# A fixed set of seven-product row pairs for every MLP product, with a new order of the weight blocks and three-part additions to x

## The chip, the cores and the metric

The kernel runs on one core of a Trainium2 chip. The metric is the device time of one execution in microseconds (us); where several runs are given, the median counts. Engines: PE is TensorE (matmuls), DVE is VectorE, ACT is ScalarE, POOL is GpSimd, SP issues the DMAs of the weights.

## The reference

A decoder trunk of two layers over 256 rows of 2048 float32 values: a retention layer and a latent-attention layer, each followed by an MLP. The MLPs are what the change is about:

```
def rms_norm(x, gain):
    return x * rsqrt(mean(x * x) + 1e-6) * gain

def sq_relu_mlp(h, w1, w2):            # w1: 2048 x 8192, w2: 8192 x 2048
    return square(relu(h @ w1)) @ w2

for layer in range(2):
    x = x + (retention(h) if layer == 0 else mla_attention(h))   # h = rms_norm(x, ...)
    x = x + sq_relu_mlp(rms_norm(x, norm_mlp[layer]), mlp_w1[layer], mlp_w2[layer])
```

## The kernel before, in words

**Splitting.** Every float32 operand is split into a high part (rounded to fp32r) and a low part, the rest. `split` (L182) does it: ScalarE casts (L185), VectorE subtracts (L186). A product of two operands is three matmuls: high by high, high by low, low by high (L354 to L356).

**Pair products.** `gemm_pair` (L331) multiplies the 256 rows of activations by one *column pair* of a weight: 1024 columns. The inner dimension is taken in *row pairs* of 256 weight rows. `quad` (L282) handles one row pair: it loads one 1 MB chunk (128 partitions x 2048 values, four blocks of 512 columns b11, b22, b12, b21, L285) and multiplies the 2 x 2 blocks of the activations by the 2 x 2 blocks of the weight. An *eight* does it in eight products of 128 x 128 by 128 x 512 and splits the chunk in two halves of 1024. A *seven* does it in seven products, in Strassen's manner (Winograd's form): it splits b11 with b22, then b21 alone, then adds blocks in place on VectorE (L319, L322, L323) and splits the four results u1 to u4 in two halves. It also needs sums of the activation's blocks, made beforehand by `with_sums` (L390): three subtractions or additions, and a split.

Split weights lie in rings of five buffers each, "wh" and "wl", of 128 x 1024; raw chunks lie in a ring of four. The accumulators c11, c12, c21, c22 take the four banks "acc" of PSUM, p1 and p5 the two banks "tp" that the transposes use too, p6 and p7 the two banks "at". When a pair product ends, `pair_out` (L366) copies six of them out on ScalarE (L371) and combines p1, p5, p6, p7 on VectorE: L373, L374, and one tick later L377, L378.

**The MLP.** `mlp` (L782) works in four groups of 2048 hidden columns. A group has two pair products of w1, called U1 and U2 here (p even and p odd; tiles named u_), of 8 row pairs each, and then two of w2, D1 and D2 (tiles named d_), of 8 row pairs each, over the group's eight hidden tiles. When a U ends, `up` adds the two parts of each block (`summed`, L387), scales and clips (L795), transposes on TensorE (L205), squares (L804), splits, and makes four hidden tiles; those that meet a seven get their sums at once (L807). So U1's hidden tiles are made during U2, and U2's during D1. In the first three groups the results of D1 and D2 go to x in DRAM by accumulating DMAs on POOL's queue, two parts for each of four blocks of each row half (`to_home`, L145). In the last group they are added on VectorE to x in SBUF (`into_x`, L152; L461), and, in layer 0, squared, transposed and split for the next stage while D2 runs. In layer 1 the last D2 is done by plain products with whole hidden tiles (L824).

**Which row pairs are sevens.** THREE is (3, 5, 7), FOUR is (1, 3, 5, 7), HEAD is (2, 4, 6, 7), counted from 0. U1 has FOUR (layer 0's first U1 the last two of THREE, layer 1's first U1 all of THREE); U2 has THREE. D1 has THREE; D2 has FOUR in the first three groups and THREE in layer 0's last. So a group has 4 + 3 + 3 + 4. The retention stage's pair products, whose tiles are named rp_, use HEAD already.

**Order.** A list of steps due at a clock that counts row pairs (`later`, `tick`, L99 to L110) sets the order of the program's text; the framework orders the instructions of each engine by it, and waits are by semaphores. In the trace, steps of a pair product's end stand interleaved with the next one's splits.

Of the kernel before, what the change touches and what calls it, by code (L numbers as in the profile page):

```python
# [20 lines left out]
P = 128  # L21
# [47 lines left out]
def yoco(ctx: ExitStack, tc: tile.TileContext, a):  # L69
# [212 lines left out]
    def quad(w, chunk, x, mm, name):  # L282
# [11 lines left out]
        def parts(src, n, part):  # L294
# [3 lines left out]
            return [[i[:, j * 512 : (j + 1) * 512] for i in (wh, wl)] for j in range(n)]  # L298

        if more is None:  # L300
            b11, b22 = parts(raw[:, 0:1024], 2, 0)
# [4 lines left out]
            b12, b21 = parts(raw[:, 1024:], 2, 1)  # L306
# [5 lines left out]
        b11, b22 = parts(raw[:, 0:1024], 2, 0)  # L312
# [5 lines left out]
        b = raw.rearrange("p (i n) -> p i n", i=4)  # L318
        nc.vector.tensor_tensor(  # L319
            b[:, 0:3:2], b[:, 0:2], b[:, 2].unsqueeze(1).to_broadcast([P, 2, 512]), op=ALU.add  # L320
        )
        nc.vector.tensor_tensor(b[:, 1], b[:, 0], b[:, 1], op=ALU.add)  # L322
        nc.vector.tensor_tensor(b[:, 3], b[:, 1], b[:, 3], op=ALU.add)  # L323
# [7 lines left out]
    def gemm_pair(w, chunk0, act, kinds, name, done):  # L331
# [26 lines left out]
        for i in range(len(kinds)):  # L358
# [3 lines left out]
            if i == len(kinds) - 1:  # L362
                queue.append((clock[0] + 1, -1, lambda: pair_out(made, name, done)))
            tick()

    def pair_out(c, name, done):  # L366
# [9 lines left out]
        def rest():  # L376
            nc.vector.tensor_tensor(v, o["p5"], v, op=ALU.subtract)  # L377
            nc.vector.tensor_tensor(o["p5"], o["p5"], u, op=ALU.subtract)  # L378
            done([[(o["c11"], o["p1"]), (o["c12"], v)], [(o["c21"], u), (o["c22"], o["p5"])]])
# [48 lines left out]
    def x_block_t(blocks, b, g0s, outs, name, sums):  # L428

        for k2 in range(2):  # L430
# [3 lines left out]
            for g0, out in zip(g0s, outs):  # L434
# [5 lines left out]
                elif 2 * b + k2 in FOUR:  # L440
# [341 lines left out]
    def mlp(layer, act, r, done):  # L782
        w1, w2 = a[f"mlp_w1_{layer}"], a[f"mlp_w2_{layer}"]
        f0 = 0
        for gi, nf in enumerate(GROUPS):
            hid, blocks = [], []
            last = gi == len(GROUPS) - 1

            def up(c, p, hid=hid, blocks=blocks, last=last):
# [7 lines left out]
                def turn(i):  # L797
                    for q in (2 * i, 2 * i + 1):
# [8 lines left out]
                        blocks.append((v, with_sums(u, name) if len(blocks) in (THREE if last else FOUR) else None))  # L807
# [376 lines left out]
```

## Time and profile before

| what | value |
|---|---|
| median of 3 runs | 2479.52 us (2478.8 to 2480.16) |
| the profiled execution's own time | 2477.67 us |
| its span, first to last instruction | 2475.9 us |
| granted TensorE clock | 1.00 |
| layer 0's MLP in the trace | about 729 to 1409 us |
| layer 1's MLP in the trace | about 1792 to 2471 us |

The views used below: the page (busy time of the engines, 40 slices, the chain of work that ended last); windows (busy time of each engine in a stretch, with the number of instructions in brackets); groups of instructions (line, engine, operation, out<-in, shapes, count, busy time in us, mean duration of one in ns, idle time before them and what ended it); the timeline (start, duration, instruction; equal neighbours are merged, with a count; in square brackets the engine's idle time before it and what ended that); and waits. Instructions of one engine overlap a little, so a group's busy time is below count times mean.

### The profile page before, as it was taken

To read this page: it belongs to the slowest core of one execution; us is meant where nothing else is said; L and a number is where in the kernel's file an instruction comes from. 1 tells how busy PE (TensorE), PEld (TensorE's weight loads), DVE (VectorE), ACT (ScalarE), POOL (GpSimd) and SP (SyncE) were. 2 spreads that over 40 slices of the span, in tenths; PEclk is the share of its full clock that TensorE was granted. 3 is DMA by queue.
4 is the path that set the end of the run, shared out by engine and by line. 5 is a ranking of instruction groups with operands and counts; after the bars stand their busy time and mean duration, and the time that the engine had idled before them with its cause. 6 is when DMAs were issued, how large, how long until landed. Compare 5 with 4: busy or idle time off the path is not lost.

```text
span 2475.9 us, 31725 instructions
## 1 busy us (share of the span) xinstructions
PE 2457.9 (99%) x11638; PEld 2061.5 (83%) x11638; DVE 2158.9 (87%) x2800; ACT 1592.6 (64%) x2251; POOL 249.6 (10%) x310
## 2 busy tenths in 40 slices
PE   9999999999999999999999999999999999999999
PEld 7888888888888888888888888998888888888887
DVE  7799989889899999999999967776689999999996
ACT  6566655555676667667666766576566666676663
POOL 7400011000000010110110001110000201101100
PEclk9999999999999999999999999999999999999999
DMA  9645468556564685674785564445645956857854
GB/s 324 214 173 206 172 207 253 189 184 220 195 226 182 211 265 210 208 259 174 245 266 203 187 231 166 157 154 174 199 173 203 261 214 206 269 201 222 270 192 153
DMA packets 93404, 521.05 MB, mean 210 GB/s; under 512 B 11072, under 2 KB 12224, under 8 KB 40000
## 3 DMA queue, kind: packets, MB, share of 16 engines
q1 hardware_dynamic: 71856, 472.83, 53.0%
q0 software_dynamic: 21248, 46.15, 9.0%
q8 instruction: 91, 1.49, 0.2%
q14 instruction: 65, 0.53, 0.1%
q10 hardware_dynamic: 144, 0.05, 0.0%
HBM read 479.14 MB, written 39.85 MB: 210 GB/s over the span
## 4 chain that ended last, share of the span: by engine, by line
PE 93%; DVE 4%; ACT 2%; issue 1%; POOL 1%; DMA 0%; SPq 0%; ACTq 0%; DVEq 0%; POOLq 0%
PE u_c L354 7%; PE u_c L356 7%; PE u_c L355 7%; PE d_c L356 6%; PE d_c L354 6%; PE d_c L355 6%; PE rp_c L354 3%; PE rp_c L355 3%; PE rp_c L356 2%; PE rk_acc L274 2%; PE rq_acc L274 2%; PE u_p L354 2%; PE u_p L356 2%; PE u_p L355 2%; PE d_p L354 2%; PE d_p L356 2%
## 5 line engine op out<-in xcount | busy, mean ns | idle before, releaser
L185 ACT CAST u_wh<-u_raw 128x1024 fp32r<-128x1024 f32 x362 | 342.2, 990 | 214.1 <-DVE u_raw L322 155.3
L185 ACT CAST d_wh<-d_raw 128x1024 fp32r<-128x1024 f32 x358 | 337.9, 992 | 203.8 <-DVE d_raw L322 164.3
L186 DVE TENSOR_TENSOR u_wl<-u_raw,u_wh 128x1024 fp32r<-128x1024 f32 x362 | 396.8, 1143 | 52.0 <-ACT u_wh L185 50.7
L186 DVE TENSOR_TENSOR d_wl<-d_raw,d_wh 128x1024 fp32r<-128x1024 f32 x358 | 392.4, 1145 | 42.0 <-ACT d_wh L185 41.5
L354 PE MATMUL u_c<-u_wh,n 128*128 128x512 f32 x706 | 276.4, 392 | 0.0
L355 PE MATMUL u_c<-u_wl,n 128*128 128x512 f32 x706 | 275.6, 390 | 0.0
L356 PE MATMUL u_c<-u_wh,n 128*128 128x512 f32 x706 | 274.9, 389 | 0.0
L354 PE MATMUL d_c<-d_wh,hid 128*128 128x512 f32 x654 | 256.0, 391 | 0.0
L355 PE MATMUL d_c<-d_wl,hid 128*128 128x512 f32 x654 | 255.3, 390 | 0.0
L356 PE MATMUL d_c<-d_wh,hid 128*128 128x512 f32 x654 | 254.7, 389 | 0.0
L185 ACT CAST rp_wh<-rp_raw 128x1024 fp32r<-128x1024 f32 (+1 forms) x166 | 158.9, 981 | 147.1 <-DVE rp_raw L322 73.1
L186 DVE TENSOR_TENSOR rp_wl<-rp_raw,rp_wh 128x1024 fp32r<-128x1024 f32 (+1 forms) x166 | 182.5, 1136 | 31.1 <-ACT rp_wh L185 29.5
L356 PEld LDWEIGHTS u_c<-u_wh,n 128*128 128x128 f32 x706 | 132.6, 188 | 27.5
L354 PEld LDWEIGHTS u_c<-u_wh,n 128*128 128x128 f32 x706 | 132.6, 188 | 26.9
L355 PEld LDWEIGHTS u_c<-u_wl,n 128*128 128x128 f32 x706 | 132.6, 188 | 26.6
L356 PEld LDWEIGHTS d_c<-d_wh,hid 128*128 128x128 f32 x654 | 122.8, 188 | 25.4
L354 PEld LDWEIGHTS d_c<-d_wh,hid 128*128 128x128 f32 x654 | 122.8, 188 | 25.0
L355 PEld LDWEIGHTS d_c<-d_wl,hid 128*128 128x128 f32 x654 | 122.9, 188 | 24.8
L150 POOL DMA_DIRECT2D xh<-d_c x48 | 41.6, 867 | 856.1 <-ACT d_c L371 854.2
L185 ACT CAST ro_wh<-ro_raw 128x1024 fp32r<-128x1024 f32 x86 | 83.1, 998 | 59.0 <-DVE ro_raw L322 30.4
L354 PE MATMUL rp_c<-rp_wh,a 128*128 128x512 f32 x286 | 112.0, 392 | 1.1 <-DVE rk_u L624 1.1
L356 PE MATMUL rp_c<-rp_wh,a 128*128 128x512 f32 x286 | 111.4, 390 | 0.0
(465 smaller groups left out, 6070.7 us busy)
## 6 DMA issues: line engine op xcount, KB each, us to landing
u_raw<-in_mlp_w SPq DMA_DIRECT2D x128, 1024.0 KB, 5.7
d_raw<-in_mlp_w SPq DMA_DIRECT2D x120, 1024.0 KB, 5.1
rp_raw<-in_ret_w_gv SPq DMA_DIRECT2D x56, 1024.0 KB, 4.9
ro_raw<-in_ret_w_out SPq DMA_DIRECT2D x32, 1024.0 KB, 4.8
uq_raw<-in_mla_w_uq SPq DMA_DIRECT2D x24, 768.0 KB, 4.1
rq_raw<-in_ret_w_qk SPq DMA_DIRECT2D x16, 1024.0 KB, 5.2
rk_raw<-in_ret_w_qk SPq DMA_DIRECT2D x16, 1024.0 KB, 4.8
wo_raw<-in_mla_w_o SPq DMA_DIRECT2D x16, 1024.0 KB, 4.8
```

Source lines behind the costliest of these rows:

```text
L150: nc.gpsimd.dma_start(x_home[t][2 * p + j], part, accum_op=ALU.add)
L185: nc.scalar.copy(h, src)
L186: nc.vector.tensor_tensor(l, src, h.bitcast(F32), op=ALU.subtract)
L274: nc.tensor.matmul(acc[f], wh[:, cols], a.rearrange("p i s -> p (i s)"), start=k == 0, stop=k == nk - 1)
L354: nc.tensor.matmul(dst, ah, bh, start=n == 0, stop=False)
L355: nc.tensor.matmul(dst, ah, bl, start=False, stop=False)
L356: nc.tensor.matmul(dst, al, bh, start=False, stop=n == total[key] - 1)
```

## The change

Five things, all in the MLPs' pair products or in `quad`, which the retention stage's pair products use too.

1. Every pair product of the MLPs takes HEAD, row pairs 3, 5, 7, 8 counted from 1, as its sevens: 4 + 4 + 4 + 4 in a group. The exceptions are layer 0's first U1 (row pairs 7, 8) and layer 1's first U1 (5, 7, 8), and layer 1's last D2, which is as it was. The sums of x's blocks that U needs are made for HEAD too.
2. The weight's blocks lie as b11, b12, b22, b21. An eight splits blocks 0 and 2, then 1 and 3; a seven splits 0 and 2, then 3.
3. In a seven the first add gives u1 and u3 together, the second u2, the third u4. The splits are u1 with u3, then u2 with u4; the products go p5, p7, p6, c21.
4. In the first three groups, D1's and D2's results leave L377 and L378 out: ScalarE negates u and v, and the blocks of the second column half go to x in three parts.
5. The sums of hidden tiles are separate steps: of tile k, due max(k - 4, 0) ticks after the tile. `blocks` is now a `Pairs` (L25), whose length counts a tile that needs sums when they are there.

```diff
-            wh = pool.tile([P, 1024], F32R, tag="wh", bufs=5, name=f"{name}_wh{part}")
-            wl = pool.tile([P, 1024], F32R, tag="wl", bufs=5, name=f"{name}_wl{part}")
-            split(wh[:, : n * 512], wl[:, : n * 512], src)
+            n = src.free_size() // 512
+            wh, wl = (
+                pool.tile([P, 2, 512], F32R, tag=f"w{i}", bufs=5, name=f"{name}_w{i}{part}")[:, :n] for i in "hl"
+            )
+            split(wh, wl, src)
...
+        b11, b22 = parts(b[:, 0:3:2], 0)
         if more is None:
...
-            b12, b21 = parts(raw[:, 1024:], 2, 1)
+            b12, b21 = parts(b[:, 1:4:2], 1)
...
-        (b21,) = parts(raw[:, 1536:], 1, 1)
+        (b21,) = parts(b[:, 3:4], 1)
         mm("c11", a(0, 1), b21)
         nc.vector.tensor_tensor(
-            b[:, 0:3:2], b[:, 0:2], b[:, 2].unsqueeze(1).to_broadcast([P, 2, 512]), op=ALU.add
+            b[:, 0:2], b[:, 0:3:2], b[:, 1].unsqueeze(1).to_broadcast([P, 2, 512]), op=ALU.add
         )
-        nc.vector.tensor_tensor(b[:, 1], b[:, 0], b[:, 1], op=ALU.add)
-        nc.vector.tensor_tensor(b[:, 3], b[:, 1], b[:, 3], op=ALU.add)
-        u1, u2 = parts(raw[:, 0:1024], 2, 2)
+        nc.vector.tensor_tensor(b[:, 2], b[:, 0], b[:, 2], op=ALU.add)
+        nc.vector.tensor_tensor(b[:, 3], b[:, 2], b[:, 3], op=ALU.add)
+        u1, u3 = parts(b[:, 0:2], 2)
         mm("p5", s(1), u1)
+        mm("p7", s(0), u3)
+        u2, u4 = parts(b[:, 2:4], 3)
         mm("p6", s(2), u2)
-        u3, u4 = parts(raw[:, 1024:], 2, 3)
-        mm("p7", s(0), u3)
         mm("c21", a(1, 1), u4)
...
         def rest():
+            if loose:
+                less = f2k([512], f"{name}_n")
+                nc.scalar.activation(less, u, AF.Copy, scale=-1.0)
+                nc.scalar.activation(v, v, AF.Copy, scale=-1.0)
+                done([[(o["c11"], o["p1"]), (o["c12"], o["p5"], v)], [(o["c21"], u), (o["c22"], o["p5"], less)]])
+                return
             nc.vector.tensor_tensor(v, o["p5"], v, op=ALU.subtract)
             nc.vector.tensor_tensor(o["p5"], o["p5"], u, op=ALU.subtract)
...
-                elif 2 * b + k2 in FOUR:
+                elif 2 * b + k2 in HEAD:
...
-            hid, blocks = [], []
+            hid, sums = [], []
             last = gi == len(GROUPS) - 1
+            kinds = HEAD
+            blocks = Pairs(hid, sums, kinds)
...
-                        blocks.append((v, with_sums(u, name) if len(blocks) in (THREE if last else FOUR) else None))
+                        k = len(hid)
                         hid.append(v)
+                        sums.append(None)
+                        if k in kinds:
+                            def sum_up(k=k, u=u, name=name):
+                                sums[k] = with_sums(u, name)
+                            later(max(k - 4, 0), sum_up)
...
-                kinds = THREE[not (p or layer) :] if p % 2 or not p else FOUR
+                sevens = HEAD if p else HEAD[2 - layer :]
...
-                kinds = [i in (FOUR if p and not last else THREE) for i in range(2 * nf)]
-                gemm_pair(w2, p * 32 + 2 * f0, blocks, kinds, f"d{layer}_{gi}{p}", add)
+                gemm_pair(
+                    w2, p * 32 + 2 * f0, blocks, [i in kinds for i in range(2 * nf)], f"d{layer}_{gi}{p}", add, not last
+                )
...
-    w = np.stack([w[:, :, :, 0, 0], w[:, :, :, 1, 1], w[:, :, :, 0, 1], w[:, :, :, 1, 0]], axis=3)
+    w = np.stack([w[:, :, :, 0, 0], w[:, :, :, 0, 1], w[:, :, :, 1, 1], w[:, :, :, 1, 0]], axis=3)
```

More of the change, by code (lines that the diff above doesn't have):

```diff
@@ L362, in gemm_pair, with pair_out @@
             if i == len(kinds) - 1:
-                queue.append((clock[0] + 1, -1, lambda: pair_out(made, name, done)))
+                queue.append((clock[0] + 1, -1, lambda: pair_out(made, name, done, loose)))
             tick()
-    def pair_out(c, name, done):
+    def pair_out(c, name, done, loose):
         o = {}
@@ L785, in mlp, with up @@
         for gi, nf in enumerate(GROUPS):
-            hid, blocks = [], []
+            hid, sums = [], []
             last = gi == len(GROUPS) - 1
-            def up(c, p, hid=hid, blocks=blocks, last=last):
+            kinds = HEAD
+            blocks = Pairs(hid, sums, kinds)
+            def up(c, p, hid=hid, sums=sums, kinds=kinds):
                 need(r, NT)
@@ L813, in mlp @@
             for p in range(f0 // 2, (f0 + nf) // 2):
-                kinds = THREE[not (p or layer) :] if p % 2 or not p else FOUR
+                sevens = HEAD if p else HEAD[2 - layer :]
                 gemm_pair(
-                    w1, p * 8, act, [i in kinds for i in range(8)], f"u{layer}_{p}", lambda c, p=p, up=up: up(c, p)
+                    w1, p * 8, act, [i in sevens for i in range(8)], f"u{layer}_{p}", lambda c, p=p, up=up: up(c, p)
                 )
```

10 lines of the change are left out of this document (4 added, 6 removed).

## The prediction

> **What bounds the kernel now.** I read the page first: the busy line, the slices, the chain of work that ended last.
>
> ```profile
> span 2475.9 us, 31725 instructions
> PE 2457.9 (99%) x11638; PEld 2061.5 (83%) x11638; DVE 2158.9 (87%) x2800; ACT 1592.6 (64%) x2251; POOL 249.6 (10%) x310
> DVE  7799989889899999999999967776689999999996
> PE 93%; DVE 4%; ACT 2%; issue 1%; POOL 1%; DMA 0%; SPq 0%; ACTq 0%; DVEq 0%; POOLq 0%
> ```
>
> TensorE (PE) holds 93% of the chain. VectorE (DVE) is at 87% on average, but at nine tenths in most slices of the two MLP stretches, so the question is what it has left where the change puts work. An MLP group is four pair products of 8 row pairs each: U1, U2 (w1) and D1, D2 (w2). The timeline of TensorE where a U2 ends and a D1 begins gives the rate of a matmul and the place of the boundary (start, duration):
>
> ```profile
> 985.02 0.39 PE L354 MATMUL u_c<-u_wh,n 128*128 128x512 f32 x1
> 985.25 0.39 PE L355 MATMUL u_c<-u_wl,n 128*128 128x512 f32 x1
> 985.47 0.39 PE L356 MATMUL u_c<-u_wh,n 128*128 128x512 f32 x1
> 985.70 0.39 PE L354 MATMUL d_c<-d_wh,hid 128*128 128x512 f32 x1
> ```
>
> Matmuls start every 0.227 us, 0.68 us for a product's three. Then the windows of one pair product each: of a retention pair, U1, U2, D1, D2 of layer 0's second group, and layer 0's last D2 (length, then PE, PEld, DVE, ACT, POOL busy, clock, DMA share):
>
> ```profile
> 597.80:640.60 42.80, 42.72 (x191) 35.04 (x190) 38.16 (x48) 24.29 (x31) 0.00 (x0) 1.00 0.48 176
> 901.40:942.20 40.80, 40.80 (x182) 33.74 (x181) 37.96 (x41) 25.01 (x31) 4.37 (x5) 1.00 0.83 263
> 942.20:985.70 43.50, 43.50 (x200) 35.86 (x199) 41.17 (x52) 31.12 (x43) 0.00 (x0) 1.00 0.53 190
> 985.70:1029.20 43.50, 43.50 (x200) 35.89 (x199) 41.20 (x52) 31.14 (x43) 2.59 (x3) 1.00 0.53 188
> 1029.20:1070.10 40.90, 40.90 (x182) 33.82 (x181) 38.07 (x41) 25.09 (x31) 6.99 (x8) 1.00 0.87 261
> 1366.60:1409.20 42.60, 42.60 (x193) 35.11 (x192) 41.45 (x53) 28.86 (x45) 2.17 (x4) 1.00 0.54 185
> ```
>
> TensorE is never idle in the MLP windows. VectorE is busy 38 of 41 us in U1 and D2, which have four sevens, and 41.2 of 43.5 in U2 and D1, which have only three: there it also does the combining, the halves' sums and the hidden tiles of the U before. U2 and D1 are the heavy pairs, with 2.3 us of VectorE to spare.
>
> **What the change takes from TensorE.** A seven saves one product. Counted from the code: 26 + 27 sevens in w1 now, 30 + 31 after; 27 + 24 in w2 now, 32 + 28 after. The first add of each seven has its own row, and the counts agree:
>
> ```profile
> L319 DVE TENSOR_TENSOR u_raw<-u_raw 128x1024 f32<-128x1024 f32 x53 | 64.6, 1219 | 0.0
> ...
> L319 DVE TENSOR_TENSOR d_raw<-d_raw 128x1024 f32<-128x1024 f32 x51 | 62.2, 1219 | 0.0
> ```
>
> Seventeen more sevens, 17 x 0.68 = **11.6 us less** of TensorE. Eight are in a U2 and eight in a D1, one each per group; the last is in layer 0's last D2. U1 and other D2s keep their number.
>
> **What it puts on VectorE.** The end of D1 shows what a seven costs (timeline of VectorE):
>
> ```profile
> 1013.86 6.37 DVE L186 TENSOR_TENSOR d_wl<-d_raw,d_wh 128x1024 fp32r<-128x1024 f32 x6 [0.47 <-ACT d_wh L185]
> 1020.15 1.22 DVE L319 TENSOR_TENSOR d_raw<-d_raw 128x1024 f32<-128x1024 f32 x1
> 1021.40 0.69 DVE L322 TENSOR_TENSOR d_raw<-d_raw 128x512 f32<-128x512 f32 x1
> 1022.13 0.69 DVE L323 TENSOR_TENSOR d_raw<-d_raw 128x512 f32<-128x512 f32 x1
> 1023.29 3.71 DVE L186 TENSOR_TENSOR d_wl<-d_raw,d_wh 128x1024 fp32r<-128x1024 f32 x3 [0.47 <-ACT d_wh L185]
> ```
>
> The first row holds five full subtracts and a half one: (6.37 - 0.69) / 5 = 1.14 us each, and the next starts 0.60 after the half one. The adds follow at 1.25 and 0.73 when each waits for the one before, at 1.14 and 0.60 when other work stands between. An eight takes 2 x 1.14; a seven takes 1.14 + 0.60, the adds 1.14 to 1.25, 0.60 to 0.73 and 0.60, and 2 x 1.14. The difference is 4.1 to 4.3; I take **4.2**. The cast of a half block stands in ScalarE's groups:
>
> ```profile
> L185 ACT CAST d_wh<-d_raw 128x1024 fp32r<-128x1024 f32 x307 | 309.2, 1053 | 202.6 <-DVE d_raw L322 164.3 <-PE d_acc L248 16.6 <-PE d_c L356 9.7
> ```
>
> The wait of 0.47 for it goes: u1 and u3 are ready after the first add, so ScalarE casts (1.05 us) while VectorE does the other two (1.33). I count only busy time, so this needs no term: it is time that VectorE gets to use. The layout itself (strided halves of equal length) I take at nothing: this first add has a strided output already, at 1.22. If strides cost or saved 0.05 on each of 5 operations, that is 0.25 per seven, inside the range.
>
> Sums of hidden tiles, by group (means of one):
>
> ```profile
> L186 DVE TENSOR_TENSOR hid_more<-hid_sum,hid_more 128x512 fp32r<-128x512 f32 x30 | 20.6, 686 | 0.0
> ...
> L394 DVE TENSOR_TENSOR hid_sum<-hid_u 128x256 f32<-128x256 f32 x30 | 12.6, 420 | 0.0
> ...
> L378 DVE TENSOR_TENSOR d_p<-d_p,d_u 128x512 f32<-128x512 f32 x15 | 10.3, 687 | 0.0
> ...
> L396 DVE TENSOR_TENSOR hid_sum<-hid_u,hid_sum 128x128 f32<-128x128 f32 x30 | 8.6, 286 | 0.0
> ```
>
> One sum is 0.69 + 0.42 + 2 x 0.29 (L395 has L396's shape), less 0.08 overlap each: 1.34. Now U2 makes two of a group's sums and D1 two (positions 2, 4 and 6, 8). After, positions 3, 5, 7, 8 need them: one in U2, **three in D1**. Deferring the last ones by some row pairs keeps them in D1.
>
> The three-part additions take L377 and L378 (0.60 each by spacing) off VectorE and give ScalarE, busy for 25 of 41 us in such a pair, two negations. But they are of D1's result, done in D2, and of D2's, done in the next U1: the light pairs, where nothing waits for VectorE. So no gain; without them VectorE would need 38.1 of 40.9 there.
>
> **The sum, group by group.** VectorE after: U1 37.96 - 1.2 = 36.8; U2 41.17 + 4.2 - 1.34 = 44.0; D1 41.20 + 4.2 + 1.34 = 46.7; D2 38.07 - 1.2 = 36.9. TensorE: 40.8, 42.8, 42.8, 40.9. Over a group VectorE has 164.4 against 167.3 and would fit, if it could work ahead. How far it can shows before 985.70 and at the end of D1:
>
> ```profile
> 982.27 1.22 DVE L186 TENSOR_TENSOR d_wl<-d_raw,d_wh 128x1024 fp32r<-128x1024 f32 x1 [0.15 <-ACT d_wh L185]
> 984.07 1.23 DVE L186 TENSOR_TENSOR d_wl<-d_raw,d_wh 128x1024 fp32r<-128x1024 f32 x1 [0.57 <-ACT d_wh L185]
> 985.50 2.36 DVE L186 TENSOR_TENSOR d_wl<-d_raw,d_wh 128x1024 fp32r<-128x1024 f32 x2 [0.21 <-ACT d_wh L185]
> ```
>
> ```profile
> 1027.85 0.39 PE L354 MATMUL d_p<-d_wh,hid_more 128*128 128x512 f32 x1
> 1028.07 0.39 PE L355 MATMUL d_p<-d_wl,hid_more 128*128 128x512 f32 x1
> ```
>
> When TensorE starts D1, VectorE has done 1.22 + 1.23 + 0.20 = 2.65 us of D1's splits, with waits for casts between: there are five wh and five wl buffers, the ending seven holds four, and casts wait for the rest. That lead is all a light pair can hand on. At the other end the last split must be done 1.14 us before the pair ends (1028.07 against 1029.21); now it is done at 1023.29 + 1.14 + 1.22 = 1025.65, 2.4 early.
>
> After the change: U2 has 42.8 - 1.14 + 2.65 = 44.3 for 44.0, so it just fits, 0.3 early. VectorE then starts D1 only 1.4 before TensorE and has 43.1 for 46.7: **TensorE waits 3.7 us in each D1** (2.3 if the whole lead survived and a seven costs 4.1; 4.9 if half a us of other waits comes in and U2 stalls too). D2 then gives VectorE 4 us back and the lead returns, capped as before. Eight groups: 8 x 3.7 = 29.6. One new wait lies inside this one. The first seven of a heavy pair comes one row pair (5.4 us) earlier, and its p1 and p5 take the banks that the hidden tiles' transposes use. The last square that reads them in D1, and now's first p1:
>
> ```profile
> 999.87 0.60 ACT L804 ACTIVATE hid_u<-hid_tp 128x512 f32<-128x512 f32 x1
> ...
> 1004.05 0.39 PE L354 MATMUL d_p<-d_wh,hid 128*128 128x512 f32 x1
> ```
>
> p5, three products behind p1, would come at 1004.05 - 5.4 + 2.0 = 1000.6 and the square ends at 1000.47: between nothing and some 1.5 us of wait in TensorE's order, which VectorE uses to catch up. I add nothing. In U1 of each layer's first group, fewer sevens leave more room; the later order of row sums of x I take at nothing there.
>
> Layer 0's last D2 also carries the additions to x and their transposes. Its last split and the matmul that needs it:
>
> ```profile
> 1403.23 2.36 DVE L186 TENSOR_TENSOR d_wl<-d_raw,d_wh 128x1024 fp32r<-128x1024 f32 x2 [0.47 <-ACT d_wh L185]
> ```
>
> ```profile
> 1408.04 0.39 PE L355 MATMUL d_p<-d_wl,hid_more 128*128 128x512 f32 x1
> ```
>
> It is 2.45 early. One more seven (4.2), less two cast waits that vanish (0.9), plus TensorE's 0.68 less, plus the lead lost (2.65 - 1.14), less 2.45: 3.0 us of wait. Sum: 29.6 + 3.0 - 11.6 = **+21.0** on the profiled execution's 2477.67, 2498.7; the median of the runs shown stands 1.85 above it, so **2500.5**. By the bounds, 8 x 2.3 + 1.5 and 8 x 4.9 + 4 for the waits: 2488 to 2511.
>
> [...]
>
> **Rivals.** (a) VectorE keeps up, and the time falls. The engines' orders interleave pieces of several steps, as the rows above do; if U2's combining and sums come to stand so that D1 starts with a larger lead than mine, the wait per group shrinks. It decides at 11.6 / 8 = 1.45 us: D1's VectorE work under 44.5 with the lead as worked out. With no waits at all: 2479.52 - 11.6 = 2467.9. For it: VectorE's total fits over a group, and the retention window above runs four sevens in this very order (two at the end) with TensorE at 42.72 of 42.80. Against it: that window holds only 38.2 us of VectorE. Chance 0.18; another 0.10 that it half works (waits of 1.45 to 2.3, 2475 to 2488).
>
> (b) Transfers. Ten accumulating DMAs in place of eight after each D of the first three groups, three to one place of x, where each waits for the one before. The first half of D2, POOL's waits, and these DMAs' time to landing:
>
> ```profile
> 1029.20:1050.00 20.80, 20.80 (x93) 17.18 (x92) 20.27 (x23) 12.61 (x16) 4.40 (x5) 1.00 0.99 266
> ```
>
> ```profile
> POOL xh L150 <- DMA xh<-d_c: 14.5, 2, 7.3
> ```
>
> ```profile
> DMA to landing us min/median/max: 3.9/8.4/13.9
> ```
>
> The third part starts some 8 us later, so the busy stretch grows longer rather than denser: (0.87 - 0.53) x 40.9 / 8 = 1.7 us a DMA, 3.5 for two, and 0.87 x 40.9 + 3.5 = 39.1 of 40.9. Still under the pair. If weights came late by 2 us in each of the 12 light pairs, beyond the 4 us of VectorE's slack, the time would be 2525. Chance 0.07.
>
> (c) VectorE's operations no longer overlap, each waiting out the one before: U2 53 x 0.085 = 4.5 and D1 61 x 0.085 = 5.2 more. U2 then waits for 44.0 + 4.5 - 44.3 = 4.2 and D1, with no lead but the last 1.14, for 46.7 + 5.2 - 42.8 = 9.1, so 8 x 13.3 + 3.0 - 11.6 = 98 on 2479.5, some 2577. The x6 row nearly excludes it: 0.01. [...] (d) The number of sevens does not grow, 2479.5: 0.02; the lists of kinds say it does.
>
> **How the numbers follow.** Forecast 0.62, rival (a) 0.18 and 0.10, (b) 0.07, (c) 0.01, (d) 0.02. A difference under 0.2% (5 us) is about what a measurement of this kernel can't tell from none. Faster is (a): 0.18. Same (2474.6 to 2484.5) is six of the ten hundredths of the half case, and (d): 0.08. Slower: 0.74. The forecast alone holds 2488 to 2511; down to 2472 it takes in the half case and part of (a), and up to 2512 nothing of (b). About 0.18 stays outside.
>
> **What the profile would show.** Right: the first add counted 61 and 60 times; D1 windows of 45 to 48 us with VectorE over 97% busy and TensorE idle before L355 for the subtract of L186; U2 near 43; U1 and D2 as now with VectorE at nine tenths; no cast waits of 0.47 behind the third add. Wrong: TensorE idle in U1 or D2, or before a weight load for a DMA; D1 under 44.3; a seven's adds or splits off 1.14 and 0.60. What would make it wrong is a lead above 2.65 us at the start of D1, or VectorE work of D1 that I count there and that runs elsewhere.

## The result, and the profile after

| | before | after |
|---|---|---|
| median of the runs shown together | 2479.16 us (2478.31 to 2480.16, 4 runs) | 2545.32 us (2542.22 to 2545.82, 4 runs) |
| ratio, 95% interval | | 1.0267 (1.0255 to 1.0279) |
| the profiled execution's own time | 2477.67 us | 2545.73 us |

The change makes the kernel 66 us slower. The direction was predicted; the size (2500.5, and 2512 as the upper end) was not. The page of the changed kernel: span, busy time, VectorE's slices, the chain of work that ended last.

```profile
span 2543.6 us, 31798 instructions
...
PE 2485.6 (98%) x11587; PEld 2052.6 (81%) x11587; DVE 2228.6 (88%) x2869; ACT 1639.2 (64%) x2311; POOL 270.3 (11%) x334
...
DVE  7799989889989999999999967775699999999995
...
PE 67%; DVE 20%; ACT 7%; issue 4%; DMA 1%; POOL 0%; ACTq 0%; SPq 0%; DVEq 0%; POOLq 0%
```

TensorE held 93% of the chain; now VectorE holds 20% and ScalarE 7%. VectorE's share of the span is only one point higher, 88% for 87%: the average hardly moved, and the chain did. The first add of a seven, by group, of the changed kernel:

```profile
L321 DVE TENSOR_TENSOR u_raw<-u_raw 128x1024 f32<-128x1024 f32 x61 | 74.4, 1220 | 0.0
L321 DVE TENSOR_TENSOR d_raw<-d_raw 128x1024 f32<-128x1024 f32 x60 | 73.3, 1222 | 0.0
```

61 and 60, as counted; TensorE's matmuls fall from 11638 to 11587, by 51, three for each of 17 products. The windows of the changed kernel, one pair each: U1, U2, D1, D2 of layer 0's second group, then D1 and D2 of its last (length, then PE, PEld, DVE, ACT, POOL busy, clock, DMA share, GB/s):

```profile
908.30:949.60 41.30, 41.13 (x181) 33.63 (x180) 37.34 (x39) 26.58 (x33) 6.10 (x7) 1.00 0.84 261
949.60:994.70 45.10, 44.13 (x197) 34.92 (x197) 44.26 (x53) 32.05 (x44) 0.00 (x0) 1.00 0.52 187
994.70:1042.80 48.10, 44.70 (x197) 34.99 (x196) 46.92 (x61) 33.26 (x47) 2.59 (x3) 1.00 0.56 185
1042.80:1083.70 40.90, 40.90 (x182) 33.68 (x180) 37.17 (x39) 26.41 (x32) 8.11 (x10) 1.00 0.87 266
1345.80:1396.30 50.50, 45.48 (x193) 34.89 (x192) 48.47 (x64) 33.96 (x47) 0.00 (x0) 0.98 0.45 165
1396.30:1442.10 45.80, 43.71 (x191) 34.66 (x189) 44.31 (x56) 29.18 (x47) 2.17 (x4) 0.99 0.50 179
```

VectorE's busy times, 37.3, 44.3, 46.9 and 37.2, are those of the prediction (36.8, 44.0, 46.7, 36.9) within 0.6 us. But U2 lasts 45.1 against 42.8 of TensorE's own, D1 48.1 against 42.8, U1 41.3 against 40.8: TensorE loses 2.3, 5.3 and 0.5, some 8.1 us in a group where 3.7 was predicted. D2 loses nothing. What TensorE waits for in the changed kernel's MLPs (us in total, times, longest):

```profile
PE d_c L356 <- ACT d_wh L185: 16.7, 17, 1.3
PE d_p L356 <- ACT d_wh L185: 7.8, 16, 1.7
...
PE d_p L357 <- DVE d_wl L186: 4.2, 14, 0.5
PE u_c L356 <- ACT u_wh L185: 3.6, 8, 0.5
```

Most waits name ScalarE's cast of a weight block. The timeline of the third row pair of D1, where the changed kernel has its first seven, shows what the casts waited for. TensorE:

```profile
1010.29 0.73 PE L356 MATMUL d_p<-d_wh,hid_more 128*128 128x512 f32 x2 [0.35 <-ACT d_wh L185]
1012.28 0.50 PE L356 MATMUL d_c<-d_wh,hid 128*128 128x512 f32 x1 [1.26 <-ACT d_wh L185]
1012.94 0.50 PE L357 MATMUL d_p<-d_wl,hid_more 128*128 128x512 f32 x1 [0.16 <-DVE d_wl L186]
```

ScalarE, the same stretch:

```profile
1009.19 1.04 ACT L185 CAST d_wh<-d_raw 128x1024 fp32r<-128x1024 f32 x1
1010.13 0.63 ACT L185 CAST hid<-hid_u 128x512 fp32r<-128x512 f32 x1
1011.18 2.95 ACT L185 CAST d_wh<-d_raw 128x1024 fp32r<-128x1024 f32 x3 [0.42 <-DVE d_raw L325]
```

VectorE, the same stretch:

```profile
1006.88 1.23 DVE L321 TENSOR_TENSOR d_raw<-d_raw 128x1024 f32<-128x1024 f32 x1
1008.32 0.69 DVE L186 TENSOR_TENSOR hid_more<-hid_sum,hid_more 128x512 fp32r<-128x512 f32 x1 [0.21 <-ACT hid_more L185]
1008.92 0.69 DVE L186 TENSOR_TENSOR hid<-hid_u,hid 128x512 fp32r<-128x512 f32 x1
1009.52 0.69 DVE L324 TENSOR_TENSOR d_raw<-d_raw 128x512 f32<-128x512 f32 x1
1010.13 0.42 DVE L403 TENSOR_TENSOR hid_sum<-hid_u 128x256 f32<-128x256 f32 x1
1010.46 0.69 DVE L325 TENSOR_TENSOR d_raw<-d_raw 128x512 f32<-128x512 f32 x1
```

Follow it back. TensorE at 1012.28 waits for a cast; that cast waited until 1011.18 for the third add (L325); the add ran at 1010.46, because VectorE, without a pause longer than 0.21 us, had put the hidden tiles' splits and sums of U2 between the seven's three adds. This wait is named after ScalarE, and VectorE makes it. The smaller wait before it, at 1010.29, is ScalarE's own: the first add (L321) was done at 1008.11, but the cast of its results ran at 1009.19, behind ScalarE's squares and casts for U2's hidden tiles. In the same window of D1 there are smaller stalls behind the fifth row pair (some 0.75 us) and the eighth (1.7).

How full VectorE is inside D1 is seen when the window is cut. Before the change, the first three row pairs and the other five:

```profile
985.70:1003.80 18.10, 18.10 (x88) 14.87 (x87) 17.82 (x28) 14.02 (x23) 0.00 (x0) 1.00 0.50 187
1003.80:1029.20 25.40, 25.40 (x113) 21.02 (x112) 23.38 (x24) 17.13 (x21) 2.59 (x3) 1.00 0.55 189
```

The changed kernel, cut inside the third row pair, where TensorE has come to the end of its wait:

```profile
994.70:1013.30 18.60, 16.81 (x79) 12.92 (x78) 18.39 (x28) 15.27 (x25) 0.00 (x0) 1.00 0.44 166
1013.30:1042.80 29.50, 27.88 (x120) 22.07 (x119) 28.53 (x34) 18.00 (x23) 2.59 (x3) 1.00 0.64 196
```

Before, VectorE had 2.3 us to spare in D1, but 2.0 of them in the last 25.4 us and only 0.3 in the first 18.1, where the combining, the halves' sums and U2's first hidden tiles stand. The change puts a seven into that first stretch. VectorE gets through 28 operations in either kernel, and TensorE through 79 matmuls; the three row pairs hold 85 now (88 before, less the three that the seven saves), so the last of them are still to come.

### The profile page after: what moved, and what is told of

The parts are those of the page before. It is cut to its first block, busy times and chain, and to the rows that moved or that the text cites. A ratio compares the mean times of both kernels' runs of the same rounds, so it can differ in the third digit from the quotient of the medians.

```text
span 2543.6 us, 31798 instructions
## 1 busy us (share of the span) xinstructions
PE 2485.6 (98%) x11587; PEld 2052.6 (81%) x11587; DVE 2228.6 (88%) x2869; ACT 1639.2 (64%) x2311; POOL 270.3 (11%) x334
## 4 chain that ended last, share of the span: by engine, by line
PE 67%; DVE 20%; ACT 7%; issue 4%; DMA 1%; POOL 0%; ACTq 0%; SPq 0%; DVEq 0%; POOLq 0%
DVE u_wl L186 5%; PE d_c L356 4%; PE u_c L357 4%; PE d_c L357 4%; PE d_c L358 4%; PE u_c L358 4%; PE u_c L356 4%; DVE d_wl L186 4%; PE rp_c L356 2%; PE rp_c L357 2%; PE rp_c L358 2%; PE rq_acc L274 2%; PE rk_acc L274 2%; PE ro_c L357 2%; PE ro_c L358 2%
## 5 line engine op out<-in xcount | busy, mean ns | idle before, releaser
L185 ACT CAST u_wh<-u_raw 128x1024 fp32r<-128x1024 f32 x378 | 358.9, 986 | 213.9 <-DVE u_raw L321 148.8
L185 ACT CAST d_wh<-d_raw 128x1024 fp32r<-128x1024 f32 x376 | 355.2, 985 | 169.9 <-DVE d_raw L321 94.6
L186 DVE TENSOR_TENSOR u_wl<-u_raw,u_wh 128x1024 fp32r<-128x1024 f32 x378 | 415.9, 1135 | 47.8 <-ACT u_wh L185 43.4
L186 DVE TENSOR_TENSOR d_wl<-d_raw,d_wh 128x1024 fp32r<-128x1024 f32 x376 | 414.2, 1137 | 35.1 <-ACT d_wh L185 31.5
L356 PE MATMUL u_c<-u_wh,n 128*128 128x512 f32 x658 | 259.0, 394 | 3.6 <-ACT u_wh L185 3.6
L357 PE MATMUL u_c<-u_wl,n 128*128 128x512 f32 x658 | 258.0, 392 | 2.4 <-DVE u_wl L186 2.4
L358 PE MATMUL u_c<-u_wh,n 128*128 128x512 f32 x658 | 257.1, 391 | 0.0
L356 PE MATMUL d_c<-d_wh,hid 128*128 128x512 f32 x600 | 229.8, 397 | 16.7 <-ACT d_wh L185 16.7
L358 PE MATMUL d_c<-d_wh,hid 128*128 128x512 f32 x600 | 235.2, 392 | 0.0
L357 PE MATMUL d_c<-d_wl,hid 128*128 128x512 f32 x600 | 234.8, 391 | 0.1
L356 PEld LDWEIGHTS d_c<-d_wh,hid 128*128 128x128 f32 x600 | 113.8, 190 | 47.2 <-ACT d_wh L185 24.4
L357 PEld LDWEIGHTS u_c<-u_wl,n 128*128 128x128 f32 x658 | 123.5, 188 | 34.1 <-DVE u_wl L186 8.3
L356 PEld LDWEIGHTS u_c<-u_wh,n 128*128 128x128 f32 x658 | 123.5, 188 | 33.5 <-ACT u_wh L185 8.6
L358 PEld LDWEIGHTS u_c<-u_wh,n 128*128 128x128 f32 x658 | 123.6, 188 | 25.0
L357 PEld LDWEIGHTS d_c<-d_wl,hid 128*128 128x128 f32 x600 | 113.5, 189 | 24.8 <-DVE d_wl L186 0.5
L358 PEld LDWEIGHTS d_c<-d_wh,hid 128*128 128x128 f32 x600 | 113.2, 189 | 23.3
```

The costliest lines, as they stand in the source:

```text
L185: nc.scalar.copy(h, src)
L186: nc.vector.tensor_tensor(l, src, h.bitcast(F32), op=ALU.subtract)
L356: nc.tensor.matmul(dst, ah, bh, start=n == 0, stop=False)
L357: nc.tensor.matmul(dst, ah, bl, start=False, stop=False)
L358: nc.tensor.matmul(dst, al, bh, start=False, stop=n == total[key] - 1)
```

## The experiments

The kernel before ran on the same chips as these, at 2478.07 to 2478.87 us. Ratios are to it. Windows are of layer 0's second group where nothing else is said. The theory to start with (A): the loss is made by the fourth sevens in U2 and D1, through VectorE, and the lead that a light pair hands on is too small. The rival (B): the new layout, the order in a seven, the later sums or the three-part additions cost it. The later rivals W (the amount of work in U2 and D1 decides, wherever it stands) and E (the seven in the third row pair decides) came out of the first eight runs.

### Which part of the change

**old_kinds**: the change with the former choice of sevens; layout, order in a seven, three-part additions and deferred sums stay.

```diff
-                sevens = HEAD if p else HEAD[2 - layer :]
+                sevens = THREE[not (p or layer) :] if p % 2 or not p else FOUR
...
-[i in kinds for i in range(2 * nf)]
+[i in (FOUR if p and not last else THREE) for i in range(2 * nf)]
```

(The sums of x's blocks and of the hidden tiles follow the same choice.)

> The changed kernel with the row pairs that were sevens before (4, 3, 3, 4 in a group; no two next to each other), the sums of hidden tiles still deferred, layout, order inside a seven and three-part additions as changed. Theory A (VectorE has too much work in the second w1 product and the first w2 product of a group, and two sevens in a row at a pair's end leave it no lead: 0.7 us at the start of U2 instead of 2.65): the waits go, 2474 to 2483 us. Theory B (the other parts cost the time: the seven's new order, which puts matmuls on the high parts of later products ahead, the deferral, or the three-part additions): still over 2500 us.

Measured: 2479.79 us, ratio 1.0006 (0.9997 to 1.0015). With the former sevens, everything else costs nothing and gains nothing. Theory B falls, as far as this run can tell: here VectorE is ahead.

**two_part**: the additions to x in two parts again.

```diff
-            if loose:
+            if False:
```

> The changed kernel with the two-part additions to x of before in place of the three-part ones: 1.2 us more on VectorE in U1 and D2, two negations less on ScalarE, eight accumulating DMAs in place of ten. Theory A: U1 and D2 have 3.7 us to spare, so 2541 to 2549 us, as the changed kernel. If the additional DMAs or ScalarE's negations cost time: under 2538 us.

Measured: 2544.0 us, 1.0266 (1.0251 to 1.0281), the same as the changed kernel. The VectorE time that three parts save lies in the light pairs, where TensorE loses 0.5 us in U1 and nothing in D2.

### Which pairs pay

**heavy3**: three sevens (row pairs 5, 7, 8) in U2 and D1, four in U1 and D2. **light3**: the reverse. But for the layers' first and last pairs both have the same number of sevens.

```diff
-                sevens = HEAD if p else HEAD[2 - layer :]
+                sevens = (HEAD[1:] if p % 2 else HEAD) if p else HEAD[2 - layer :]
...
-[i in kinds for i in range(2 * nf)]
+[i in (HEAD if p else HEAD[1:]) for i in range(2 * nf)]
```

and for light3:

```diff
-                sevens = HEAD if p else HEAD[2 - layer :]
+                sevens = (HEAD if p % 2 else HEAD[1:]) if p else HEAD[2 - layer :]
...
-[i in kinds for i in range(2 * nf)]
+[i in (HEAD[1:] if p else HEAD) for i in range(2 * nf)]
```

heavy3:

> The changed kernel with three sevens (row pairs 5, 7, 8) in U2 and D1 and four (3, 5, 7, 8) in U1 and D2: 14 a group as before, two neighbours still at the end of every pair. Theory A (U2 and D1 together are bound by VectorE's work, 91.2 us plus some 2 of idle time, after the change): their work falls by 8.4 us, U2 fits TensorE's 43.5 and D1 is over it by under 1; a group is 169 to 171 us and the whole 2479 to 2492 us. If the neighbours at the end cost the time: over 2510 us.

light3:

> The changed kernel with three sevens (row pairs 5, 7, 8) in U1 and D2 and four (3, 5, 7, 8) in U2 and D1: 14 a group as before, and the same work for VectorE and TensorE in all as heavy3. Theory A: U2 and D1 take 93 us as in the changed kernel, U1 and D2 0.7 us more each, so 2543 to 2555 us. If the total of VectorE's work or the number of sevens decided: near heavy3's time, under 2495 us.

Measured: heavy3 2497.85 us, 1.0081 (1.0066 to 1.0096), somewhat over what was expected; light3 2549.68 us, 1.0286 (1.0271 to 1.0301), as expected. Almost the same work, 52 us apart. One thing heavy3 shows beside this: its second group lasts 170.1 us, and that of the kernel before 168.7 (the sum of its four windows), with 4, 3, 3 and 4 sevens in both. So the places of the sevens, two of them side by side at the end, cost some 1.4 us a group even where their number is the former one. The windows of light3, U1 to D2:

```profile
908.70:950.40 41.70, 41.54 (x183) 33.97 (x182) 32.90 (x34) 24.66 (x31) 6.14 (x7) 1.00 0.86 259
950.40:995.80 45.40, 44.41 (x199) 35.19 (x198) 44.53 (x53) 32.32 (x44) 0.00 (x0) 1.00 0.52 185
995.80:1044.30 48.50, 46.02 (x198) 36.36 (x197) 47.05 (x61) 33.20 (x47) 2.59 (x3) 0.96 0.55 183
1044.30:1085.70 41.40, 41.40 (x184) 34.09 (x183) 32.79 (x34) 24.54 (x30) 8.05 (x10) 1.00 0.91 263
```

VectorE is free for almost 9 us in each light pair, and U2 and D1 are as long as in the changed kernel. Spare time of a light pair buys the heavy one nothing: over a group VectorE has 157.3 us of work in 177.0, and TensorE still waits.

**u2_three** and **d1_three**: only one of the two heavy pairs gets three sevens; the first diff below is u2_three, the second d1_three.

```diff
-                sevens = HEAD if p else HEAD[2 - layer :]
+                sevens = (HEAD[1:] if p % 2 else HEAD) if p else HEAD[2 - layer :]
```

```diff
-[i in kinds for i in range(2 * nf)]
+[i in (HEAD if p else HEAD[1:]) for i in range(2 * nf)]
```

u2_three:

> Only U2 goes back to three sevens (row pairs 5, 7, 8; in the two first groups too); D1 keeps four. Theory W: U2 and D1 share VectorE, so taking 4.2 us off either gives half of the 6.2 us that U2 + D1 grew: about 2545 - 8 x 3.1 = 2520 (2514 to 2526). Theory E (each pair pays for its own third row pair): U2 goes from 45.1 to 43.5 and D1 stays at 48.1, 2545 - 8 x 1.6 = 2532 (2528 to 2537).

d1_three:

> Only D1 goes back to three sevens (row pairs 5, 7, 8); U2 keeps four. Theory W: as with U2 alone, about 2520 (2514 to 2526). Theory E: D1 goes from 48.1 to 43.5 and U2 stays at 45.1, 2545 - 8 x 4.6 = 2508 (2503 to 2513).

Measured: u2_three 2530.34 us, 1.0208 (1.0191 to 1.0225); d1_three 2503.63 us, 1.0098 (1.0083 to 1.0113). These are 15 and 42 us less than the changed kernel: near theory E's 13 and 37, not theory W's 25 each. So each heavy pair pays for its own fourth seven, and D1 pays nearly three times what U2 does. Together they would give 57; heavy3, which has both edits, gives 47. The rest overlaps, and I did not follow it up. The windows of U2 and D1 in d1_three:

```profile
944.10:989.20 45.10, 44.15 (x197) 34.93 (x196) 44.21 (x53) 32.01 (x44) 0.00 (x0) 1.00 0.53 186
989.20:1033.00 43.80, 43.80 (x201) 35.87 (x200) 42.54 (x56) 31.57 (x44) 2.62 (x3) 1.00 0.59 199
...
989.20:1007.50 18.30, 18.30 (x90) 15.06 (x89) 18.30 (x27) 15.96 (x25) 0.00 (x0) 1.00 0.72 265
```

D1 without the seven in its third row pair has no wait at all, at 42.54 us of VectorE in 43.80, behind an unchanged U2; the stalls behind its fifth and eighth row pair have gone as well, though these are sevens still: they hung on the third's. The last row is the first stretch of this D1: VectorE is busy in all of its 18.30 us, and TensorE does not wait. So a full stretch alone is not yet a wait. My reading is that it becomes one when what TensorE needs next stands in it behind more work than VectorE's lead covers.

**last_old**: only the last groups' D pairs go back to row pairs 4, 6, 8.

```diff
-            kinds = HEAD
+            kinds = THREE if last else HEAD
             blocks = Pairs(hid, sums, kinds)
```

> Only the D pairs of each layer's last group go back to row pairs 4, 6, 8 (as in the kernel before); all else as in the changed kernel. The last groups grew by 13.3 and 11.8 us, against 6 to 7 of the others, and the stage behind layer 0's by 2.6. If the extra is the added sevens of layer 0's last D2 and the two last D1, D falls from 96.3 to about 88 and from 96.8 to about 89, U keeps its 2.1: 2545 - 18 = 2527 (2522 to 2533). If it comes from the neighbours (the lead, the clock), less than 10 comes back: over 2535.

Measured: 2523.81 us, 1.0183 (1.0168 to 1.0198), 21.5 us less than the changed kernel. The windows of D1 and D2 in layer 0's last group:

```profile
1346.20:1390.00 43.80, 43.80 (x201) 35.94 (x200) 42.53 (x55) 31.34 (x44) 0.00 (x0) 1.00 0.53 193
1390.00:1434.00 44.00, 43.21 (x193) 34.95 (x192) 42.99 (x55) 29.78 (x46) 2.17 (x4) 1.00 0.57 196
```

D1 was 50.5 and D2 45.8 there. A third of the whole loss stood in the last groups' D pairs, and the sevens there made it; the run changes their number and their places together and does not tell the two apart.

### Whether the place inside a pair matters

**mid**: row pairs 3, 4, 6, 8 in place of 3, 5, 7, 8, so that a pair ends in an eight and a seven, as before. **late4**: row pairs 4, 5, 6, 8. The number of sevens is that of the change.

```diff
+MID, LATE = (2, 3, 5, 7), (3, 4, 5, 7)
...
-                elif 2 * b + k2 in HEAD:
+                elif 2 * b + k2 in MID:
...
-            kinds = HEAD
+            kinds = MID
...
-                sevens = HEAD if p else HEAD[2 - layer :]
+                sevens = MID if p else MID[2 - layer :]
```

(late4 has LATE in these places.)

mid:

> The changed kernel with row pairs 3, 4, 6, 8 as sevens in place of 3, 5, 7, 8: as many sevens, but the two neighbours stand early in the pair and an eight stands before the last seven; two hidden sums fall into U2 and two into D1 in place of one and three. Theory A: the lead at the start of U2 is back near 2.65 us and D1 has one sum (1.34 us) less, so a group waits some 5.6 us in place of 8.1: 2520 to 2530 us. Number alone (the place of the sevens does not matter): 2540 to 2548 us. Theory B: the same 2540 to 2548.

late4:

> Row pairs 4, 5, 6, 8 as sevens everywhere in the MLPs, in place of 3, 5, 7, 8: the same number of sevens and the same VectorE work in U2 and D1 (91.2 us), but the first seven of a heavy pair comes a row pair later, behind the hidden tiles of the U before, and a light pair ends in an eight and a seven as in the kernel before. Theory W (what is lost follows VectorE's work in U2 and D1 together, wherever the sevens stand): U2 + D1 stay near 93, 2538 to 2552. Theory E (the seven in the third row pair, whose chain of adds, casts and subtracts falls between the end of the last pair and the hidden tiles, is what costs): only what the amount alone makes is lost, 91.2 less the 2.65 of lead against 85.6, some 3 us a group in place of 8.1, so about 2545 - 8 x 4.9 = 2506 (2498 to 2515).

Measured: mid 2550.43 us, 1.0291 (1.0276 to 1.0306), so the better end of a light pair did not help, and theory A's figure was missed; late4 2574.02 us, 1.0379 (1.0362 to 1.0395), slower than either theory had it. U2 and D1 of mid:

```profile
950.00:998.70 48.70, 45.84 (x198) 36.14 (x197) 45.88 (x57) 33.10 (x45) 0.00 (x0) 0.96 0.49 176
998.70:1045.20 46.50, 44.17 (x197) 34.81 (x196) 45.29 (x57) 32.20 (x45) 2.46 (x3) 1.00 0.50 168
```

And of late4, first U1, U2 and D1 whole, then a stretch of D1 from inside its fourth row pair to the end of the sixth:

```profile
909.30:952.00 42.70, 41.50 (x182) 33.59 (x181) 37.38 (x39) 26.32 (x33) 6.09 (x7) 1.00 0.88 257
952.00:996.90 44.90, 43.64 (x197) 35.00 (x196) 43.96 (x53) 32.08 (x44) 0.00 (x0) 1.00 0.55 186
996.90:1047.80 50.90, 46.51 (x197) 35.90 (x196) 47.09 (x61) 33.58 (x46) 2.62 (x3) 0.97 0.52 174
...
1018.00:1038.30 20.30, 15.91 (x56) 10.73 (x55) 18.77 (x22) 11.51 (x14) 0.00 (x0) 0.92 0.43 142
```

VectorE's work in U2 and D1 together is 91.2 us in the changed kernel and in mid, and 91.1 in late4; the two pairs last 93.2, 95.2 and 95.8. So theory W falls: with the same amount, the place matters. In mid the lead is back: when TensorE starts U2, at 950.03, VectorE has done 2.66 us of its splits (subtracts at 946.60, 948.40 and 949.83). TensorE still waits 2.9 us in the fourth row pair of U2, the second of two sevens side by side, and a stretch at half the clock follows (the mean clock of U2's window is 0.96).

In late4 the first 21 us of D1 run without a wait, and then three sevens in a row stop TensorE for over 4 us in 20. Each hands TensorE 4.77 us of work (seven products of 0.68) and takes 6.5 of VectorE (the prediction's prices: 2 x 1.14, 4.2 more), so 1.7 are lost for each, and a few us of lead are soon used up. Even the light U1 of late4 lasts 42.7 us for 41.3 in the changed kernel and waits at its sixth row pair, the third of three sevens, though VectorE is busy for only 37.4 of the 42.7. So theory E in its narrow form falls: the third row pair is no special place. What fits all these runs is that any stretch of some ten us costs time in which VectorE has more to do than TensorE: the first 18 us of a heavy pair with a seven added, or sevens one behind another.

### Whether it is VectorE's work

**no_summed** leaves out the eight additions of the two parts of a U's results (so the hidden tiles are made of one part); in the heavy pairs' first stretch 4.8 us a group go.

```diff
-                c = summed(c)
+                c = [[block[0] for block in row] for row in c]
```

> The changed kernel without the four additions of the w1 products' parts (it leaves this part of the computation out: the hidden tiles are made of one part alone), which takes 4 x 0.60 us off VectorE in U2 and in D1 and nothing off TensorE. Theory A: U2 and D1 are bound by VectorE, so each of the 8 groups gets 4.8 us shorter until TensorE binds: 2500 to 2515 us. If the waits come from the sevens' own chain (add, cast, subtract) or from the order of TensorE's matmuls, and not from the amount: over 2530 us.

Measured: 2518.67 us, 1.0163 (1.0146 to 1.018); a group takes 172.0 us where the changed kernel takes 175.4, 3.4 of the 4.8. That is 4 us over theory A's range and far below the rival's 2530: the amount of VectorE's work is worth most of its length here.

**pool_all** gives combining, halves' sums and hidden tiles' sums of the U's to GpSimd.

```diff
+            eng = nc.gpsimd if name[0] == "u" else nc.vector
+            eng.tensor_tensor(v, o["p5"], v, op=ALU.subtract)
+            eng.tensor_tensor(o["p5"], o["p5"], u, op=ALU.subtract)
...
-                c = summed(c)
+                c = summed(c, nc.gpsimd)
...
-                                sums[k] = with_sums(u, name)
+                                sums[k] = with_sums(u, name, nc.gpsimd)
```

> The changed kernel with part of VectorE's work of U2 and D1 on GpSimd, which is idle there: the two last combinations of a w1 product, the four additions of its parts, and the three small operations of each hidden sum (6 x 0.60 us and 0.74 us or more a sum, so 4.4 us off U2 and 5.8 off D1). Theory A: VectorE then has 39.9 us of work in U2 and 41.1 in D1 against TensorE's 42.8, the waits fall from 8.1 us a group to under 2, 2470 to 2495 us. Theory B: stays over 2520 us. A third possibility: GpSimd's operations (1.39 us for 128x512 in the sine tables) slow VectorE's or come too late for the transposes, 2495 to 2530 us.

Measured: 2635.73 us, 1.0637 (1.0621 to 1.0653), the slowest of all. D1 of pool_all:

```profile
1012.80:1066.80 54.00, 45.88 (x198) 36.06 (x197) 48.11 (x46) 33.30 (x46) 22.16 (x18) 0.97 0.47 161
```

VectorE has 46 operations in place of 61 and is busy longer, 48.11 us for 46.92. The first add in a stretch of 80 us that holds D1, in the changed kernel:

```profile
L321 DVE TENSOR_TENSOR d_raw<-d_raw 128x1024 f32<-128x1024 f32 x7 | 8.6, 1222 | 0.0
```

and in pool_all:

```profile
L321 DVE TENSOR_TENSOR d_raw<-d_raw 128x1024 f32<-128x1024 f32 x4 | 5.9, 1486 | 0.0
```

The same operation takes 1486 ns on average for 1222, in a D1 where GpSimd is busy for 22.16 us in place of 2.59. But TensorE's longest waits are others: the hidden tiles come late. Its transposes wait for ScalarE's step before them (the waits of TensorE):

```profile
PE hid_tp L205 <- ACT u_c L808: 42.0, 16, 2.6
```

and that step waits 112.6 us for GpSimd's additions of 1.7 to 2.3 us each; two further waits, 47.7 us together, stand at the products that need the banks of the transposes. So this run is no test of how much VectorE work matters; it shows that GpSimd is no place for it in this kernel.

**rings6**: six split buffers in each ring for five, paid for with three raw chunks for four.

```diff
-        raw = pool.tile([P, 2048], F32, tag="raw", bufs=4, name=f"{name}_raw")
+        raw = pool.tile([P, 2048], F32, tag="raw", bufs=3, name=f"{name}_raw")
...
-                pool.tile([P, 2, 512], F32R, tag=f"w{i}", bufs=5, name=f"{name}_w{i}{part}")[:, :n] for i in "hl"
+                pool.tile([P, 2, 512], F32R, tag=f"w{i}", bufs=6, name=f"{name}_w{i}{part}")[:, :n] for i in "hl"
```

(The same numbers are changed where the other stages take from these rings.)

> The changed kernel with six buffers in place of five for split weights, and three in place of four for raw chunks, to make room. Theory A: each light pair can hand on one more tile, up to 1.14 us of lead, so 1 to 2 us less wait in a group: 2529 to 2538 us. Theory B: no change, 2542 to 2548 us. If the missing raw chunk makes the weights late, slower than the changed kernel and VectorE or ScalarE waits for DMAs of raw chunks.

Measured: 2556.32 us, 1.0315 (1.0298 to 1.0332). The casts now wait for weights (the waits of ScalarE):

```profile
ACT d_wh L185 <- DMA d_raw<-in_mlp_w: 26.8, 11, 3.9
```

D2 lasts 43.9 us there for 40.9, while U2 and D1, at 44.9 and 47.9, are each 0.2 us shorter. The missing raw chunk costs more than the buffers give, so whether a longer ring alone would help stays open. No version of the twelve beats the kernel before; old_kinds equals it.

## Why the prediction was right or wrong

**TensorE's saving: right.** 61 and 60 sevens, 51 matmuls fewer.

**VectorE's work in each pair: right** within 0.6 us (the windows above), and D1 at 48.1 us has VectorE 97.5% busy, as the test for it said. Two signs failed: "U2 near 43" (45.1), and TensorE idle before L355 (now L357) for the subtract. In the D pairs 24.5 us of its waits stand one matmul earlier, for the cast, and 4.2 at the subtract. The prices of a seven and of a sum hold. The cast wait goes in part: VectorE's waits for casts in the D pairs came 54 times where they had come 90 times. Layout and three-part additions: nothing, as said (old_kinds, two_part).

**The failed step: "U2 has 42.8 - 1.14 + 2.65 = 44.3 for 44.0, so it just fits", and the same sum for D1.** It takes a pair as one budget, with one lead handed over at its start. It gave TensorE no wait in U2 and 3.7 us in D1; the runs showed 2.3 and 5.3. Two things are wrong in it.

First, the lead. I read 2.65 us from the kernel before, whose U2 ends in an eight and a seven. After the change every pair ends in two sevens, 13 us of VectorE in 9.5 of TensorE. VectorE before U2, in the changed kernel:

```profile
948.91 2.36 DVE L186 TENSOR_TENSOR u_wl<-u_raw,u_wh 128x1024 fp32r<-128x1024 f32 x2 [0.69 <-ACT u_wh L185]
```

and TensorE where U2 begins:

```profile
949.64 0.39 PE L356 MATMUL u_c<-u_wh,n 128*128 128x512 f32 x1
950.19 0.50 PE L357 MATMUL u_c<-u_wl,n 128*128 128x512 f32 x1 [0.16 <-DVE u_wl L186]
```

949.64 - 948.91 = 0.73 us of lead, and TensorE waits at once. With 0.73 my own sum gives 42.8 - 1.14 + 0.73 = 42.4 for U2's 44.0, a wait of 1.6, where 2.3 was measured. D1 then starts with 1.14 and waits 3.9. So the right lead brings a group from 3.7 to 5.5, of 8.1 measured.

Second, the budget. mid and late4 have the former end of a light pair, and they are slower. In mid the lead is 2.66 us; my sum with VectorE's measured 45.9 in U2 would be 45.9 less 44.3, a wait of 1.6, and U2 lasts 48.7, that is 5.9 over TensorE's 42.8 (at most 1.7 of it the half clock, by the estimate in the last section). VectorE's spare time counts only in the stretch where it lies: of D1's 2.3 us, 0.3 lay in the first 18.1, and the seven was put there. By the pair the wait is 46.7 less 43.1; stretch by stretch it is 2.7 us in the third row pair alone, and the fifth and eighth pay again. d1_three, with that one seven out, has no wait in D1; its 42.54 us would fit by the pair too, so it shows the cost of that seven and not which of the two sums is right. The light U1 of late4, which waits with 5 us of VectorE free in the pair, speaks for the stretch.

**The sum, by its terms.** Growth from start to start, in the two profiled executions: six groups 39.7 us together (6.0 to 7.0 each) where 2.3 each, 14, was predicted; layer 0's last group 13.3 for 4.7; layer 1's last 11.8 for 2.3; the stages between the layers 2.6 for nothing. That is 67.4 for 21.0; the profiled executions differ by 68.1. So 26 of the 46 missing us are the six groups' waits, and 18 the last groups. There I priced D1 like any other. In layer 0's its VectorE work is 48.47 (46.92 elsewhere), three additions to x among it, and the pair is 50.5 - 42.8 = 7.7 over TensorE's own time, a stretch at half the clock included (1393.8 to 1396.3, clock 0.50). last_old takes 21.5 off.

**"p5 at 1000.6: between nothing and 1.5 us; I add nothing": right** in that form. In the changed kernel p1 of D1's first seven waits some 0.3 us for the square that reads the bank; the price of the early seven was in VectorE's order instead.

**The rivals.** (a) VectorE does keep up over a group, as I said in its favour; light3 shows that this is no argument. (b) fell: D2 and U1 lose at most 0.5 us, and no engine's wait names a DMA of an MLP weight in the changed kernel. (c) fell: in the 2.36 us row above two subtracts of 1.22 overlap, and the first add is as long as before (1220 and 1222 ns for 1219). Its 0.085 us is the mean overlap in the prediction's rows: 1.22 less 1.14 for a full operation, 0.69 less 0.60 for a half one. (d) fell with the counts.

**What stays open.** How the 2.7 us of the third row pair divide between the amount of VectorE's work, its order and ScalarE's order: a version that keeps the hidden tiles' pieces out from between the seven's adds was not tried. TensorE's own order in a seven changed too (high parts of p5, p7 and c21 stand ahead of p5's low part); old_kinds has that order and loses nothing, so it costs nothing where VectorE is ahead, but it was not tried alone where VectorE is behind. mid loses in U2 at the fourth row pair; why it loses more there and the change more in D1 was not found.

## What to carry to other kernels

Add up a second engine's work over the length that its buffers can carry, here some two or three row pairs (10 to 18 us, an estimate from the windows above), and not over a loop body: an average of 95% can hide a stretch that is full. Before work is added, cut the window until the spare time's place is known, and put the work there; and read a lead for the order that will be, not for the one that was. Where a wait names an engine that is itself waiting, follow it one step further before choosing what to relieve.

## What the runs showed of the hardware

**TensorE's clock.** In the changed kernel the granted clock falls to one half (0.50 and 0.51 in their windows) in five stretches of 3.4 us, from 837.4, 1189.0, 1393.8, 1666.85 and 2110.6, and one of 6.8, from 2489.5; before, it is 1.00 from the start to 2475.6 us, past the last matmul. In late4 it is seen by the matmuls: 0.39 us long and 0.23 apart before, then

```profile
1034.61 0.61 PE L358 MATMUL d_p<-d_wh,hid_more 128*128 128x512 f32 x1
1035.02 0.63 PE L356 MATMUL d_p<-d_wh,hid_more 128*128 128x512 f32 x1
```

0.43 apart, until 1038.0 (the window of 20.3 us above, which holds them, has a mean clock of 0.92). The 3.4 us before that stretch and the 3.4 before those, in late4:

```profile
1027.80:1031.20 3.40, 3.25 (x13) 2.37 (x13) 3.37 (x5) 0.63 (x2) 0.00 (x0) 1.00 0.60 169
1031.20:1034.60 3.40, 1.75 (x6) 1.16 (x7) 3.31 (x4) 2.99 (x4) 0.00 (x0) 1.00 0.34 142
```

So this fall came without a long pause: the second window held 6 matmuls, of 15 that fit at 0.227 us each, and its longest gap was 1.08 us. In the changed kernel TensorE is busy for 0.96 to 1.98 us of the 3.4 ahead of each fall, but a window with 1.87 (2281.3 to 2284.7) was followed by none (clock 1.00 to 2288.1), so what sets off a fall was not shown. If TensorE is the bound in it, a stretch costs up to 1.7 us, an estimate: half of its 3.4 us, at half the clock. In the first three groups of each layer of the changed kernel, where VectorE is the bound in D1, D1 and D2 together last 88.7 to 88.9 us without one and 89.2 with one. By the estimate the six stretches could cost 5 x 1.7 + 3.4 = 12 us at the most; one of them lies between the layers, where the same matmuls take 4.54 us (1665.88 to 1670.42) for 2.97 before (1630.75 to 1633.72), and makes about 1.6 of the 2.6 lost there, and those in the first three groups' D1 pairs cost less than their share, 0.3 to 0.5 us each.

**GpSimd and VectorE.** In pool_all's D1, where GpSimd is busy for 22.16 of 54.00 us, the first adds of a seven, 128 x 1024, last 1486 ns on average. In the changed kernel's stretch of 80 us, whose D1 has GpSimd busy for 2.59 of 48.10 us, they last 1222. The second and third adds, 128 x 512, last 933 and 932 ns in the former and 691 and 690 in the latter. The first adds of a U in pool_all's stretch stay at 1217.
